# Moving three load buffers by 64 bytes: where an SBUF tile begins, and what the DMA engines make of it

## The chip, the cores and the metric

The kernel runs on one core of one Trainium2 chip. The metric is the device time in microseconds (us), the median of several runs of one program. Every run reported here is with a granted clock of 1.0.

## The reference

```python
def reference(x, axis):                 # x: 32 x 2048 x 2048 float32, about a tenth of it NaN; axis = -1
    return np.nanmax(x, axis=axis).astype(np.float32)
```

That is 65,536 rows of 2,048 floats: 537 MB are read, 0.26 MB are written, and the arithmetic is one pass.

## The kernel before

SBUF, the memory on the chip that the engines work in, has 128 *partitions* here. Data comes in by *tiles* of up to 28 x 512 floats per partition (57,344 bytes), into three load buffers in turn. Per piece of a tile, ACT (ScalarE) turns the upper half of every float into a 16-bit key in which NaN falls below everything, POOL (GpSimd; in some pieces ACT) writes the key back in its old form, and DVE (VectorE) takes the row maxima. The loads and stores are issued from SP (SyncE) and carried out by 16 DMA engines. All of it is hand-ordered with semaphores.

```python
    top = sing.tile([P, 1], f32, name="top")      # a bias for ACT
    warm = sing.tile([P, 1], f32, name="warm")    # loads ACT's table early: 1.28 us, done by 2.2; data from 5.8
    xts = [sing.tile([P, WIDE * D], i32, name=f"xt{i}") for i in range(BUFS)]      # 3 x 57,344 bytes
    kts = [sing.tile([P, KEYS], u16, name=f"kt{i}") for i in range(NKEYS)]         # 3 x 12,288 bytes
    accs = sing.tile([P, sum(rows)], f32, name="acc")
    # [cut]
                for c in loads:                   # one load for most tiles, several near the end
                    c *= Q
                    e = order.add("sp", nc.sync,
                        lambda: nc.sync.dma_start(
                            out=xt[:, at : at + c], in_=xg[:, base + at : base + at + c]),
                        before + lanes[turn], lane=f"load{turn}", step=16)
    # [cut: per piece ACT (Prelu) -> kt, POOL or ACT -> xt, DVE reduce -> acc]
                free[(number - 1) % BUFS] = after[-1:]    # the buffer is free after the last reduction
```

The built program lays the tiles one behind the other in each partition: four constants from byte 16,384 on, `top` at 16,512, `warm` at 16,544, and the first load buffer at 16,576, 64 x 256 + 192. The traces hold no addresses; these are those in the programs as built.

Of the kernel before, what the change touches and what calls it, by code (L numbers as in the profile page):

```python
# [49 lines left out]

KEYS = 3 * D
NKEYS = 3

LANES = 14

# [68 lines left out]
def kernel(  # L124
# [16 lines left out]
    P = nc.NUM_PARTITIONS  # L141
    f32, i32 = mybir.dt.float32, mybir.dt.int32
# [14 lines left out]
    sing = ctx.enter_context(tc.tile_pool(name="sing", bufs=1))  # L157
    flag = ctx.enter_context(
        tc.tile_pool(name="flag", bufs=1, space=bass.MemoryType.PSUM)
    )  # L160
    top = sing.tile([P, 1], f32, name="top")
    warm = sing.tile([P, 1], f32, name="warm")
    xts = [sing.tile([P, WIDE * D], i32, name=f"xt{i}") for i in range(BUFS)]
    kts = [sing.tile([P, KEYS], u16, name=f"kt{i}") for i in range(NKEYS)]
    accs = sing.tile([P, sum(rows)], f32, name="acc")
    nones = flag.tile([P, sum(rows)], i32, name="none")

    with tc.tile_critical():  # L168
# [16 lines left out]
        free = [[] for _ in range(BUFS)]  # L185
        kfree = [[] for _ in range(NKEYS)]
        key = 0
# [8 lines left out]
        for gi, (s, g) in enumerate(zip(rows, GROUPS)):  # L196
# [6 lines left out]
            for loads, pieces, reds in g:  # L203
# [26 lines left out]
                for c in pieces:  # L230
# [4 lines left out]
                    if used + c > KEYS:  # L235
                        key = (key + 1) % NKEYS
                        used = 0
                        kold, kfree[key] = kfree[key], []
                        if at + c == sum(loads) * Q:

                            kold = kold + kfree[(key + 1) % NKEYS]
                    kp = kts[key][:, used : used + c]
# [129 lines left out]
```

## Time and profile before

| what | value | how to read it |
|---|---|---|
| time | 1257.32 us (1257.19 to 1257.34, 4 runs) | these runs lie within 0.15 us; in later rounds one kernel's runs lie up to 1.0 us apart |
| DMA queue's transfer time | 99.3% of the 1255.5 us span | nearly without a pause |
| POOL, DVE, ACT busy | 93%, 89%, 79% | all below the DMA |
| full loads | 60, one every 16.940 us | the beat of the kernel up to about 1024 us |
| packets of 57,344 bytes | 7,680, median 2119 ns, mean 2120.7 ns | one DMA engine writing one partition's part of a full load |

Spacings and packet times here and below are worked out from the trace's record of every DMA packet (start, duration, size). A *packet* in that record is one descriptor: 109 loads x 128 partitions over 16 engines make 872 data packets per engine. The spacing is taken between the first packets of successive full loads.

### The profile page before, as it was taken

The numbers are of one execution on the slowest core, as the hardware profiler recorded it, in microseconds if no ns is written. First come the engines' busy times: TensorE is split into PE (matmuls) and PEld (weight loads), VectorE is DVE, ScalarE is ACT, GpSimd is POOL, SyncE is SP. The second block draws the span as 40 slices with busy tenths as digits, with TensorE's granted clock in tenths as the row PEclk, the third lists the DMA queues.
The fourth block names the chain that finished last, engine by engine and source line by source line (L and its number), as shares of the span: only waits on it lengthen the run. The fifth ranks groups of instructions, "written<-read, shape, count | busy, mean of one in ns | idle before, by whom it ended". The sixth has DMA issues, their size and how long they took to land.

```text
span 1255.5 us, 882 instructions
## 1 busy us (share of the span) xinstructions
DVE 1111.2 (89%) x180; ACT 987.6 (79%) x273; POOL 1168.4 (93%) x237
## 2 busy tenths in 40 slices
DVE  0888989888889988898988888898888899999999
ACT  3777887778787877788777877887777778889998
POOL 2999989998999899998999899989999999999997
DMA  9999999999999999999999999999999999999997
GB/s 413 438 435 413 438 438 438 437 431 418 438 438 435 435 417 438 438 435 437 435 418 438 438 433 438 420 433 438 435 437 437 417 436 426 438 428 428 426 421 281
DMA packets 16711, 537.20 MB, mean 428 GB/s; under 512 B 2752, under 2 KB 2752, under 8 KB 4160
## 3 DMA queue, kind: packets, MB, share of 16 engines
q1 hardware_dynamic: 16704, 537.14, 99.3%
q14 instruction: 7, 0.06, 0.0%
HBM read 536.87 MB, written 0.26 MB: 428 GB/s over the span
## 4 chain that ended last, share of the span: by engine, by line
DMA 42%; DVE 27%; POOL 18%; ACT 11%; SPq 1%; issue 1%; ACTq 0%
DMA xt<-in_x_dram 42%; DVE acc L180 27%; POOL xt L176 18%; ACT kt L172 10%; ACT xt L172 1%; SPq L214 1%; DVE xt L180 0%; DVE none L180 0%; SPq L367 0%; ACTq L111 0%; SPq L168 0%
## 5 line engine op out<-in xcount | busy, mean ns | idle before, releaser
L176 POOL TENSOR_SCALAR xt<-kt 128x4608 int16<-128x4608 uint16 (+10 forms) x233 | 1168.2, 5014 | 80.8 <-ACT kt L172 66.1
L180 DVE TENSOR_REDUCE acc<-xt 128x3 f32<-128x6144 f32 (+4 forms) x172 | 1108.0, 6492 | 140.4 <-POOL xt L176 130.4
L172 ACT ACTIVATE kt<-xt,top 128x3584 uint16<-128x3584 int16 (+8 forms) x252 | 937.0, 3756 | 260.6 <-DMA xt<-in_x_dram 238.8
L172 ACT ACTIVATE xt<-kt 128x3584 int16<-128x3584 uint16 (+5 forms) x19 | 51.3, 2701 | 0.6
L172 ACT ACT_TABLE_LOAD x1 | 1.3, 1283 | 0.9 <-SPq L168 0.9
L180 DVE TENSOR_REDUCE xt<-xt 128x1 f32<-128x1024 f32 x1 | 1.2, 1208 | 0.0
L180 DVE TENSOR_SCALAR none<-acc 128x428 int32<-128x428 f32 (+2 forms) x3 | 1.0, 339 | 0.1
L180 DVE TENSOR_TENSOR acc<-acc,none 128x428 int32<-128x428 int32 (+2 forms) x3 | 1.0, 332 | 0.1
L182 DVE MEMSET top<- 128x1 f32 x1 | 0.1, 59 | 1.0 <-SPq L168 1.0
L353 POOL MEMSET const-float32-0.0<- 128x1 f32 x1 | 0.1, 99 | 0.2 <-issue 0.2
L172 ACT ACTIVATE warm<-top 128x1 f32<-128x1 f32 x1 | 0.2, 202 | 0.0
L353 POOL MEMSET const-bfloat16-1.0<- 128x1 bf16 x1 | 0.1, 103 | 0.0
L353 POOL MEMSET const-uint8-127<- 128x1 uint8 x1 | 0.1, 103 | 0.0
L353 POOL MEMSET const-float32-1.0<- 128x1 f32 x1 | 0.1, 99 | 0.0
## 6 DMA issues: line engine op xcount, KB each, us to landing
xt<-in_x_dram SPq DMA_DIRECT2D x60, 7168.0 KB, 22.6
xt<-in_x_dram SPq DMA_DIRECT2D x3, 3840.0 KB, 15.1
xt<-in_x_dram SPq DMA_DIRECT2D x3, 3328.0 KB, 22.5
xt<-in_x_dram SPq DMA_DIRECT2D x8, 1024.0 KB, 27.3
xt<-in_x_dram SPq DMA_DIRECT2D x2, 4096.0 KB, 22.2
xt<-in_x_dram SPq DMA_DIRECT2D x2, 3584.0 KB, 20.3
xt<-in_x_dram SPq DMA_DIRECT2D x2, 3072.0 KB, 21.0
xt<-in_x_dram SPq DMA_DIRECT2D x3, 2048.0 KB, 31.1
```

What stands on the lines that cost most here:

```text
L172: return order.add("act", nc.scalar, lambda: nc.scalar.activation(**kw), deps)
L176: "pool", nc.gpsimd, lambda: nc.gpsimd.tensor_scalar(**kw), deps
L180: return order.add("dve", nc.vector, lambda: do(**kw), deps)
L182: e_top = order.add("dve", nc.vector, lambda: nc.vector.memset(top, EDGE), [])
L214: lambda: nc.sync.dma_start(out=xt[:, at : at + c], in_=xg[:, base + at : base + at + c]),
L353: nc = _bacc.Bacc("TRN2", target_bir_lowering=False, num_devices=1)
```

## The change

The two one-float tiles become one tile of 128 bytes, so that the three load buffers and all behind them begin on a multiple of 256 bytes. Nothing else changes.

```diff
+LEAD = 128
+
...
-    top = sing.tile([P, 1], f32, name="top")
-    warm = sing.tile([P, 1], f32, name="warm")
+
+    scalars = sing.tile([P, LEAD // 4], f32, name="scalars")
+    top, warm = scalars[:, 0:1], scalars[:, 1:2]
     xts = [sing.tile([P, WIDE * D], i32, name=f"xt{i}") for i in range(BUFS)]
```

## The prediction

> **What bounds the kernel now.** I read the page first (busy table, slices, DMA queue), then the groups by form, the chain of waits, the waits of the issuing queue, and a table of windows. The page says that three engines and the DMA are all nearly full:
>
> ```profile
> DVE 1111.2 (89%) x180; ACT 987.6 (79%) x273; POOL 1168.4 (93%) x237
> ...
> DMA  9999999999999999999999999999999999999997
> ...
> q1 hardware_dynamic: 16704, 537.14, 99.3%
> ...
> HBM read 536.87 MB, written 0.26 MB: 428 GB/s over the span
> ```
>
> The reader is to see that no compute engine reaches the share of the DMA queue: 99.3% of 1255.5 us is 1246.7 us of transfer time per DMA engine. It is a stream that hardly ever stops. The waits confirm it. Compute waits for data, and the queue waits for free buffers but early enough:
>
> ```profile
> ACT kt L172 <- DMA xt<-in_x_dram: 238.8, 66, 14.9
> DVE acc L180 <- POOL xt L176: 130.4, 57, 23.1
> POOL xt L176 <- ACT kt L172: 66.1, 72, 15.7
> ...
> SPq L214 <- DVE acc L180: 1156.9, 71, 37.9
> ```
>
> (engine and line, whom it waited for, us in total, times, longest). The issuing queue's 1156.9 us look alarming but cost nothing: a full load takes 22.6 us from issue to landing, yet loads land 16.94 us apart, so each is issued about 5.7 us before the previous one has landed, and the DMA engines go from one load straight to the next. In the steady part the timeline repeats the same pattern every 16.94 us:
>
> ```profile
> 595.56 15.15 DVE L180 TENSOR_REDUCE acc<-xt 128x4 f32<-128x8192 f32 x2 [1.79 <-POOL xt L176]
> 599.49 7.31 ACT L172 ACTIVATE kt<-xt,top 128x3584 uint16<-128x3584 int16 x2 [3.94 <-DMA xt<-in_x_dram]
> ...
> 612.50 15.15 DVE L180 TENSOR_REDUCE acc<-xt 128x4 f32<-128x8192 f32 x2 [1.80 <-POOL xt L176]
> 616.44 7.31 ACT L172 ACTIVATE kt<-xt,top 128x3584 uint16<-128x3584 int16 x2 [3.94 <-DMA xt<-in_x_dram]
> 619.81 16.77 POOL L176 TENSOR_SCALAR xt<-kt 128x3584 int16<-128x3584 uint16 x3 [0.19 <-ACT kt L172]
> ```
>
> Per tile ACT is idle 3.94 us waiting for the transfer, DVE 1.8 us, POOL 0.17 to 0.19 us. The transfer sets the pace, with POOL close behind: 16.77 us of a 16.94 us period. In one tile of eight ACT takes the 3584-element piece back from POOL (4.20 us), so POOL averages 16.77 - 4.20/8 = 16.24 us per tile. That is the real reserve, 4%.
>
> The end is different. The windows (us, then busy DVE, ACT, POOL, clock, DMA share, GB/s) show:
>
> ```profile
> 629.46:1003.00 373.54, 333.63 (x45) 288.03 (x68) 356.77 (x65) 1.00 1.00 434
> 1003.00:1130.00 127.00, 122.66 (x23) 106.01 (x29) 122.90 (x22) 1.00 1.00 428
> 1130.00:1180.00 50.00, 49.94 (x12) 49.22 (x19) 47.63 (x13) 1.00 1.00 428
> 1180.00:1230.00 50.00, 49.84 (x19) 47.01 (x27) 47.15 (x21) 1.00 1.01 422
> 1245.00:1248.00 3.00, 3.00 (x3) 3.00 (x4) 2.82 (x3) 1.00 0.27 63
> ```
>
> Until about 1130 us the DMA alone is full. From there to the end of the loads (about 1246 us) DVE is as full as the DMA (49.94 of 50). A faster transfer before 1130 us pulls this last part forward whole. A faster transfer after it mostly meets a busy DVE.
>
> [...] its packet records have a median of 312 ns for 8,192 bytes and 2119 ns for 57,344, so (2119 - 312) / (57,344 - 8,192) = 0.03676 ns per byte, 27.2 GB/s for one of 16 engines. [...] 15.15 to 15.16 us for each pair of DVE reductions through hundreds of microseconds of full transfer. I take from it that moving buffers should not change the engines' instructions.
>
> **The change part by part.** *Removed:* two tiles of one float each, which take 32 bytes apiece. With the four 32-byte constants ahead of them the first load buffer starts at byte 16,576 of a partition, 192 past a multiple of 256 (64 x 256 = 16,384). A load buffer is 57,344 = 224 x 256 bytes and a key buffer 12,288 = 48 x 256, so all of them share this phase. *Added:* one tile of 128 bytes that holds both floats: the first buffer moves up 64 bytes to 16,640 = 65 x 256, and everything behind with it. *Unchanged:* the number, form and order of instructions, the semaphores, the loads. The memset and the one-element activation at the start still act on one float. No instruction gets more elements, so compute cost is 0 us by count.
>
> What can move is one thing, the time of a load's descriptors. There are 109 loads of 128 partitions, thus 872 data descriptors per DMA engine, 480 of them of 57,344 bytes (60 full loads x 8).
>
> Size of what can be won: the first packets of successive full loads are 16.940 us apart (median from the packet records). Eight descriptors of 57,344 bytes at 27.2 GB/s are 16.866 us. The remainder is 0.074 us per load. [...]
>
> [...]
>
> The descriptors that count are those before 1130 us: the 60 full loads and about nine tiles of smaller ones, 69 x 8 = 552 (more where a tile is split, which I neglect). [...] After 1130 us I count at most another 0.5 us, because DVE is full there. The first load's arrival and the last reductions and stores keep their length.
>
> [...] I predict 1.0 us, **1256.3 us**.
>
> **The rivals.**
> *A: exactly nothing (1257.2 us).* [...]
> *B: [...] (1253 to 1254 us).* [...] Against: the first full loads, with the same placement, are spaced 16.914 us, 0.026 us closer than later ones, [...] unless the two act together. If they do act together (an ill-placed write that suffers only under load), the change could give it all.
> *C: POOL becomes the bound.* A period below about 16.8 us would meet POOL in seven of eight tiles. But the floor of the transfer alone is 16.866 us, so this cannot happen while POOL's instructions keep their length.
> *D: compute changes speed because its operands move too.* Read and written addresses of ACT, POOL and DVE all shift by 64 bytes. If POOL lost over 4% it would take the bound and time would rise by more than 1%; if it gained, nothing would be seen before 1130 us, and a little after. Nothing in the profile speaks for it: before and after the move, addresses are multiples of 64.
> *E: a larger gain than B*[...]. Against: 537.14 MB at 435.2 GB/s are 1234.2 us, and 1246.7 us of transfer time leave only 12.5 us even if every overhead vanished, 1.0% of the time. A gain over 2% from the transfer is out of reach.
>
> **Range and chances.** The three runs before lie within 0.15 us, so noise is small, and a run on another occasion may add some tenths. The upper end is rival A plus 0.5 us: 1257.8. The lower end is rival B with some of the tail's half microsecond: 1253.8. Faster by over 2% would need 25 us, twice what rival E leaves: 0.01. Slower by over 2% needs D at its worst: 0.01. Within 2%: 0.98.
>
> **What would show it right or wrong.** Right: full loads spaced slightly under 16.940 us and never under 16.866; the median of the 57,344-byte packets down from 2119 ns by 1 to 5 ns; the slope between packet sizes still 0.0368 ns per byte; POOL 3584, 4608 and 6144 pieces at 4200, 5341 and 7042 ns as before; DMA share still 99%. [...] the cap is wrong if the spacing goes under 16.866 us. The whole prediction is wrong if a compute group changes its mean by over 1%, or if the gap between transfers grows because buffers come free later.

The sum weighted three cases, one of them no gain at all with a weight of 0.4, the other two with 0.3 each; it came to about 1.1 us, taken down to 1.0. Of those two cases rival B is the larger. Two figures are estimates from the packet times: 16.866 us is eight packets of 57,344 bytes at the slope of 0.03676 ns per byte between the 312 and the 2119 ns, and 435.2 GB/s is 16 times the 27.2 of that slope.

## The result and the profile after

The changed kernel takes 1254.41 us (1254.32 to 1254.53, 4 runs) against 1257.32: **2.9 us less**, ratio 0.9977 (95% interval 0.996 to 0.9994). Ratios are the mean time of one kernel's fast runs over that of the other's in the same rounds, so not quite the ratio of the medians quoted. By the 2% verdict it is "same", but no run of one kernel comes near any run of the other.

Busy times, DMA slices and queue from the page of the kernel after:

```profile
DVE 1110.9 (89%) x180; ACT 987.4 (79%) x273; POOL 1168.2 (93%) x237
...
DMA  9999999999999999999999999999999999999996
...
q1 hardware_dynamic: 16704, 537.14, 99.3%
...
HBM read 536.87 MB, written 0.26 MB: 429 GB/s over the span
```

The engines' busy times are the same within 0.3 us. The queue's share is the same 99.3%, but of a span of 1252.5 us instead of 1255.5: the transfers take less time. The waits after (engine and line, whom it waited for, us in total, times, longest) say where the time came from:

```profile
ACT kt L175 <- DMA xt<-in_x_dram: 233.7, 61, 14.9
DVE acc L183 <- POOL xt L179: 128.1, 56, 23.0
POOL xt L179 <- ACT kt L175: 58.6, 40, 15.7
```

ACT waits 5.1 us less for data, and POOL 7.5 us less for ACT. A stretch of the steady part in the timeline after (start, us, engine and instruction, the idle time before it) shows it in one tile:

```profile
594.39 15.15 DVE L183 TENSOR_REDUCE acc<-xt 128x4 f32<-128x8192 f32 x2 [1.73 <-POOL xt L179]
598.30 7.31 ACT L175 ACTIVATE kt<-xt,scalars 128x3584 uint16<-128x3584 int16 x2 [3.92 <-DMA xt<-in_x_dram]
601.66 26.54 POOL L179 TENSOR_SCALAR xt<-kt 128x3584 int16<-128x3584 uint16 x5 [0.17 <-ACT kt L175]
...
615.20 7.31 ACT L175 ACTIVATE kt<-xt,scalars 128x3584 uint16<-128x3584 int16 x2 [3.89 <-DMA xt<-in_x_dram]
```

DVE and ACT instructions keep their 15.15 and 7.31 us; only the idle time before them shrinks by a few hundredths per tile (ACT's 3.94 to 3.89 or 3.92, DVE's 1.79 and 1.80 to 1.73 and 1.78). Tiles start 615.20 - 598.30 = 16.90 us apart. The same windows as before (us, then busy DVE, ACT, POOL, clock, DMA share, GB/s):

```profile
1130.00:1180.00 50.00, 50.00 (x12) 48.50 (x20) 47.48 (x14) 1.00 1.00 430
1180.00:1230.00 50.00, 49.93 (x20) 48.53 (x29) 47.72 (x21) 1.00 1.01 428
...
1245.00:1248.00 3.00, 2.97 (x3) 0.77 (x1) 0.63 (x1) 1.00 0.01 3
```

The loads are over before 1245 us, and DVE is busy for 50.00 and 49.93 of 50 us. The chain of work that ended last says the same for the stretch from 1130 us to the end. Before:

```profile
by line: DMA xt<-in_x_dram 49.3%; ACT kt L172 17.9%; DVE acc L180 16.2%; SPq L214 5.2%; POOL xt L176 3.5%; ACT xt L172 2.9%; issue 1.7%; DVE xt L180 0.9%; DVE none L180 0.1%; ACTq L111 0.0%
```

and after:

```profile
by line: DVE acc L183 94.1%; issue 4.4%; DVE xt L183 1.0%; DVE none L183 0.4%
```

After the change the end hangs on DVE alone.

From the packet records of both:

| | before | after |
|---|---|---|
| packets of 57,344 bytes: mean, median, share at exactly 2116 ns | 2120.7, 2119 ns, 12% | 2116.3, 2116 ns, 98% |
| packets of 8,192 bytes, median | 312 ns | 309 ns |
| excess of before, by packet size: 4,096 / 10,240 / 30,720 / 57,344 bytes | 3.7 / 3.9 / 3.8 / 4.4 ns | |
| spacing of full loads, median | 16.940 us | 16.909 us |

Two things are to be seen. The excess hardly grows with the size of the packet from 4,096 bytes on (3.6 to 5.2 ns over all these sizes), so it is not paid by the byte or by each 256 bytes. And after the change nearly every full packet has one and the same duration, while before nine in ten are scattered from 2116 to 2126 ns.

How the gain builds up, in landing times of loads counted from the landing of the first one:

| load landed | before, us | after, us | ahead, us |
|---|---|---|---|
| 5th | 67.77 | 67.66 | 0.11 |
| 21st | 339.51 | 338.51 | 1.00 |
| 41st | 678.46 | 677.11 | 1.36 |
| 61st (last full load) | 1017.90 | 1015.50 | 2.40 |
| 74th | 1127.93 | 1124.99 | 2.94 |
| 109th (last) | 1241.10 | 1237.11 | 3.98 |

The loads finish 4.0 us earlier and the kernel 2.9 us earlier. The other 1.1 us is swallowed at the end, where DVE is full. (The spacing is that of the first packet of each load, thus of the engine that is furthest ahead; a load has 16 landings in the trace, and its time here is the last of them. The 16 lie 0.41, 1.06, 1.17 and 1.77 us apart for the 5th, 21st, 41st and 61st load before, and 0.31, 0.57, 0.98 and 1.19 us after. That is why the lead grows unevenly, and by more than 0.031 us per load.)

### The profile page after: what moved, and what is told of

It reads as the page before. It is cut to its first block, busy times and chain, and to the rows that moved or that the text cites. A ratio compares the mean times of both kernels' runs of the same rounds, so it can differ in the third digit from the quotient of the medians.

```text
span 1252.5 us, 882 instructions
## 1 busy us (share of the span) xinstructions
DVE 1110.9 (89%) x180; ACT 987.4 (79%) x273; POOL 1168.2 (93%) x237
## 3 DMA queue, kind: packets, MB, share of 16 engines
q1 hardware_dynamic: 16704, 537.14, 99.3%
## 4 chain that ended last, share of the span: by engine, by line
DMA 36%; DVE 32%; POOL 21%; ACT 10%; issue 1%; SPq 0%
DMA xt<-in_x_dram 36%; DVE acc L183 32%; POOL xt L179 21%; ACT kt L175 9%; ACT xt L175 1%; DVE xt L183 0%; DVE none L183 0%; SPq L217 0%; SPq L370 0%; SPq L171 0%
## 5 line engine op out<-in xcount | busy, mean ns | idle before, releaser
L175 ACT ACTIVATE kt<-xt,scalars 128x3584 uint16<-128x3584 int16 (+8 forms) x252 | 936.8, 3755 | 256.8 <-DMA xt<-in_x_dram 233.7
```

The costliest lines, as they stand in the source:

```text
L175: return order.add("act", nc.scalar, lambda: nc.scalar.activation(**kw), deps)
```

## The experiments

The theory (**1**): the DMA engines pay for writes whose start in SBUF is off a multiple of 256. Its rivals: the joined tile did it (**2**); the key buffers and results had to move, so it is compute (**3**); the loss arises only where compute and DMA use the memory at once (**4**); it is a mismatch of source and destination (**5**). Within theory 1 the *size* is open: a price that grows with the distance from the multiple, one price wherever the start is, or something else. Twelve kernels ran, each in 5 rounds with runs of the kernel before on the same chip (bare_on has 4 timed runs).

### Where the start lies: past192, past64, past128, mult512

Edit: only the size of the shared tile, to 64, 192, 256 and 384 bytes.

```diff
-LEAD = 128
+LEAD = 64     # past192; 192: past64; 256: past128; 384: mult512
```

> The kernel after with its shared tile cut from 128 to 64 bytes, so that everything behind it begins 192 bytes past a multiple of 256, as in the kernel before. Theory 1 (the start of the load buffers costs the DMA engines time) and its rival 'compute operands moved' both expect the time of before, 1257.3 us, spacing of full loads 16.94 us. The rival 'the joined tile of two floats did it' expects 1254.4 us.

> Shared tile of 192 bytes: all begins 64 bytes past a multiple of 256. Theory 1 [...] expects a third of the loss, about 1255.4 us. [...] If only the 128-byte boundary counts: also 1257.3 us.

> Shared tile of 256 bytes: all begins 128 bytes past a multiple of 256. [...] 'Only multiples of 128 count': 1254.4 us.

> Shared tile of 384 bytes: load buffers begin at a multiple of 512 (the kernel after: at an odd multiple of 256; each of its buffers is 224 x 256 long, so all three are alike). Theory 1 with 256 as the unit: 1254.4 us, 57,344-byte packets at 2116 ns. If 512 is the unit: faster by up to 1 us.

(A price in proportion to the distance would give a third of the loss at 64, 1255.4 us, and two thirds at 128, 1256.3 us; one price wherever the start is, 1257.3 us in both.)

| start modulo 256 | time, us | ratio to before (95%) | 57,344-byte packets, mean ns | spacing, us |
|---|---|---|---|---|
| kernel before: 192 | 1257.14 | 1 | 2120.7 | 16.940 |
| past192: 192 | 1257.12 | 1.0 (0.9988 to 1.0013) | 2120.7 | 16.940 |
| past64: 64 | 1257.10 | 1.0 (0.9987 to 1.0012) | 2120.7 | 16.942 |
| past128: 128 | 1257.08 | 1.0 (0.9986 to 1.0013) | 2120.5 | 16.940 |
| mult512: 0 | 1254.34 | 0.9978 (0.9966 to 0.9991) | 2116.3 | 16.909 |

The time of the kernel before and the packets of the first row are from its own runs here and its trace above. past192 has the changed code at the old place and the old time: rival 2 falls. 64, 128 and 192 cost the same, so the loss does not follow the distance from the multiple. A multiple of 512 brings nothing over an odd multiple of 256: of the starts tried, 256 is the unit. Every load is a multiple of 2,048 bytes long, so the end of each write moves with its start; the runs do not part the two.

### Which tiles: loads_on_keys_off, keys_on_loads_off

```diff
+    sing.tile([P, 48], f32, name="pad")       # loads_on_keys_off (LEAD 128): keys and results 192 past
+    sing.tile([P, 16], f32, name="pad")       # keys_on_loads_off (LEAD 64): keys and results at a multiple
     kts = [sing.tile([P, KEYS], u16, name=f"kt{i}") for i in range(NKEYS)]
```

> Load buffers at a multiple of 256 as in the kernel after, but a pad of 192 bytes puts the key buffers and the results 192 past one, as in before. Theory 1 (only the DMA's writes matter): 1254.4 us. Rival 'key buffers and results matter': nearer to 1257.3 us.

> The opposite: load buffers 192 past a multiple of 256, key buffers and results on one. Theory 1: 1257.3 us, full loads 16.94 us apart. Rival: nearer to 1254.4 us.

With only the load buffers on multiples of 256: 1254.33 us, ratio 0.9977 (0.9964 to 0.9991). With only the keys and results on them: 1257.13 us, ratio 1.0 (0.9987 to 1.0012). The whole effect goes with the load buffers; where keys and results begin is worth nothing that these runs can show. (The profiled run of the first of the two was 1255.25 us: 64 packets over 2.2 us where the kernel after has 5, most of them around the sixth to tenth full load. Its spacing is 16.909 us from there on.)

### Without any compute: bare_on, bare_off

All activations, POOL instructions and reductions are cut. A load waits for the load three before it in the same buffer, and the stores write zeros. Their outputs are wrong, which doesn't matter for the times. `bare_off` has LEAD 64, thus 192 past.

```diff
-                [cut: the pieces, from "clean = []" to the last "after.append(e)"]
-                free[(number - 1) % BUFS] = after[-1:]
+                after = [e for _, _, e in landed]
+                free[(number - 1) % BUFS] = after
```

> The loads alone, at multiples of 256, each waiting only for the load three before it in the same buffer; no activations, no POOL, no reductions, and a memset and the stores as result (wrong on purpose). Theory 1 without any part of compute: full loads 16.90 to 16.91 us apart and packets of 2116 ns, about 1243 us.

> The loads alone with the buffers 192 past a multiple of 256 (wrong on purpose). If the loss lies in the DMA engines themselves: packets spread over 2116 to 2126 ns and about 4 us longer than the loads alone at multiples of 256. If it arises only where compute uses the same memory: the same time as those, packets at 2116 ns.

1247.25 us on multiples, 1251.06 us off them: **3.8 us apart**. The page of bare_on:

```profile
span 1245.4 us, 183 instructions
...
q1 hardware_dynamic: 16704, 537.14, 99.8%
```

and that of bare_off:

```profile
span 1249.3 us, 183 instructions
...
q1 hardware_dynamic: 16704, 537.14, 99.8%
```

The queue's share is 99.8% in both, so the longer span is longer transfers, with no engine at work beside them. Packets have means of 2116.2 and 2120.4 ns, spacings of 16.909 and 16.940 us: the figures of the full kernels. Rival 4 falls: the loss needs no compute. The 3.8 us agree with 872 packets x 4.2 ns = 3.7 us and with the 4.0 us by which the last load of the changed kernel lands earlier. My 1243 us for bare_on was a lapse: it is the transfer time of one engine alone, without start, last landing and stores.

### Source or destination: bare_src_off, bare_both_off

```diff
+                    sh = 48 if c == 28 * Q and base + at + c < s * D else 0     # 48 floats = 192 bytes
-                            in_=xg[:, base + at : base + at + c]
+                            in_=xg[:, base + at + sh : base + at + sh + c]
```

56 of the 60 full loads are shifted; the others would read past their partition's part of the input. A price for such reads: a time above the 1247.25 us of the loads alone would have spoken for one.

> The loads alone, buffers at multiples of 256, but nearly all full loads read from 192 bytes further on in the source (wrong on purpose). [...] If only writes pay: 1247.25 us.

> The loads alone with buffers 192 past a multiple of 256 and full loads read from 192 bytes further on (wrong on purpose), so that source and destination are alike within 256 bytes. If the loss is a mismatch between the two: near 1248 us (only the smaller loads, still unequal, lose). If it is the start of the write as such: 1251 us, or more if the read pays too.

With the source alone shifted: 1247.53 us, packets at a median of 2116 and a mean of 2116.1 ns, spacing 16.909 us. With both shifted: 1251.27 us, mean 2120.5 ns, spacing 16.940 us. Shifting the source does nothing to the packets in either case (0.3 and 0.2 us in the time, within the spread of those runs). The loss is no mismatch (rival 5 falls). It goes with the place of the write.

### How the loss is dealt out: one_off, past16

Each load buffer gets 256 spare bytes and begins at a chosen byte of them: (0, 192, 0) in one_off, (16, 16, 16) in past16.

```diff
-    xts = [sing.tile([P, WIDE * D], i32, name=f"xt{i}") for i in range(BUFS)]
+    wide = [sing.tile([P, WIDE * D + 64], i32, name=f"xt{i}") for i in range(BUFS)]
+    xts = [t[:, o : o + WIDE * D] for t, o in zip(wide, (0, 48, 0))]     # past16: (4, 4, 4)
```

> Only the second of the three load buffers is moved, to 192 past a multiple of 256 (through 256 spare bytes in each buffer); the other two stay on multiples. If each ill-placed descriptor pays for itself: a third of the loss, about 1255.3 us, packets into the second buffer 2116 to 2126 ns and the others at 2116 ns. If an ill-placed load also disturbs the next ones: more than half of the loss, slow packets in all three buffers.

> All three load buffers begin 16 bytes past a multiple of 256[...]. If any start off a multiple of 256 costs one and the same: 1257.1 us. [...]

(The other expectation: a time over the kernel before by 1 us or by far more.)

**one_off met neither expectation.** It takes 1254.62 us against 1257.24 for the kernel before (ratio 0.9979, 0.9966 to 0.9993), 2.6 us less where the change itself gives 2.9 and mult512 2.8. One ill-placed buffer of three costs some 0.2 to 0.3 us, a tenth of the loss and not a third, and even that is hardly clear of the noise. Its full packets: 98% at 2116 ns in all three buffers, the ill-placed one included; spacing 16.909 us. So an ill-placed write has no fixed price of its own. The loss comes when ill-placed loads follow one another.

The starts of the traces fit that. Spacings of the first full loads in bare_off, in us:

```
16.909 16.910 16.912 16.922 16.946 16.938 16.940 16.940 16.949 16.945
```

The first three are as short as with a good placement. From the fifth to the eighth on the spacing stays near 16.94, and does so in every kernel with all buffers 64, 128 or 192 past. The packets show the step more sharply: in each of these kernels the first four full loads have a median of 2116 ns, and from the fifth on 2119 to 2121 ns. (With the small first load, which is ill-placed too, five loads are free of the loss.)

The end of one_off shows the same. Its last tile comes in eleven loads, all into the ill-placed buffer. Mean packets of these loads, in ns:

| load of the last tile | 1st | 2nd | 3rd | 4th | 5th | 6th | 7th | 8th | 9th | 10th | 11th |
|---|---|---|---|---|---|---|---|---|---|---|---|
| bytes per packet | 6,144 | 10,240 | 8,192 | 2,048 | 6,144 | 6,144 | 6,144 | 4,096 | 4,096 | 2,048 | 2,048 |
| kernel after | 234.0 | 385.0 | 309.0 | 84.0 | 234.0 | 234.0 | 234.0 | 159.0 | 159.0 | 84.0 | 84.0 |
| one_off | 234.0 | 385.0 | 309.0 | 84.0 | 235.5 | 238.1 | 237.8 | 162.3 | 163.1 | 86.1 | 87.3 |
| kernel before | 237.0 | 389.1 | 313.8 | 84.8 | 240.3 | 238.2 | 237.8 | 162.3 | 163.0 | 86.1 | 87.1 |

Four ill-placed loads in a row cost nothing, the fifth a part, and from the sixth on packets are as slow as in the kernel before. An earlier tile of four loads into that buffer also costs nothing. So what counts seems to be the number of ill-placed loads in a row, some four or five, whether they bring 57,344 bytes per partition or 2,048 to 10,240. Why it takes so many, and how few well-placed loads in between keep the loss away, no run tells. Runs with two of three buffers off, or with fewer packets at a time, would be next.

**past16** takes 1258.87 us, ratio 1.0013 (1.0001 to 1.0026), 1.6 us more than the kernel before. Packets have a mean of 2122.7 ns, 2.0 ns over those of the kernel before and 6.4 over those of the kernel after, and 872 x 2.0 ns = 1.7 us. A start 16 bytes past a multiple costs a little more than the others tried, and not by the byte: the mean is 2.1 ns over the kernel before at 6,144 and at 10,240 bytes, and 2.0 at 57,344. Here only the first two full loads have a median of 2116 ns. The engines do not mind: from its page,

```profile
span 1256.9 us, 882 instructions
...
DVE 1111.3 (88%) x180; ACT 987.9 (79%) x273; POOL 1167.9 (93%) x237
```

busy times are those of the kernel before within 0.5 us.

No run beats the kernel after clearly; mult512 and loads_on_keys_off equal it.

## Why the prediction was right or wrong

**The bound** held: a change that touches only the transfers moved the time, and bare_on and bare_off show the transfers' 1247 and 1251 us as the floor under 1254 and 1257.

**The cost per byte** did not move: it is (2116 - 309) / 49,152 = 0.03676 ns after the change, as before, and the excess is flat over packet sizes. That only a cost per descriptor could be won back was the assumption, not shown beforehand.

**"Compute cost is 0 us by count"** held: busy times within 0.3 us, the POOL pieces of 3584, 4608 and 6144 elements at 4200, 5341 and 7039 ns. Rivals C and D of the prediction did not occur.

**The cap** held. The spacing fell to 16.909 us, not under 16.866 (an estimate from the slope), which gives back 0.031 us of the remainder of 0.074 us, 3.9 ns per descriptor; the mean packet fell by 4.4 ns.

**The term that was mis-sized** is the placement's share of that remainder: the weighting came to about 1 us, and the measured gain is 2.9, the size of the largest case, which I gave 0.3. The equal size is in part luck: that case took 552 descriptors at a price that no trace showed, while 74 x 8 = 592 had run when the lead reached 2.9 us, and full packets lost 4.4 ns. Two steps led there. First, the price per packet in the middle case was too small, and only assumed: the packets lost 4.4 ns. A price that grows with the distance from the multiple was no better: 64, 128 and 192 cost the same. Second, I read the shorter spacing of the first loads (16.914 us, 0.026 us or 3.3 ns per packet less) as a sign of something else than the placement, "unless the two act together". The exception was the truth. The first loads with a bad placement are fast because too few ill-placed ones have gone before, as the first loads of every such trace and the last ones of one_off suggest, and with a good placement the later ones are as fast (16.909).

**The end** was right in kind: the loads gained 2.9 us by the 74th, which is also the gain of the whole, and the further 1.0 us that they gained until the last one brought nothing. I had allowed it up to half a microsecond.

One reading in the prediction holds only in part: POOL's 16.24 us per tile, a reserve of 4%, is that of the first 48 full loads. In the last 12, ACT takes no piece back, and POOL has 16.77 us of each period; it still did not become the bound.

## What to carry to other kernels

Where a kernel is bound by its loads, try load buffers that begin on multiples of 256 bytes (and are multiples of 256 long, so that all share the start): here it cost 64 bytes and brought 2.9 us of 1257, a quarter of a per cent but clear of the noise. Look at the scatter of equal packets in the trace: here 98% had one duration with the good placement and 12% with the bad. Look at packets by load, not only at their mean: that the loss starts with the fifth load tells more than its size. And the last part of this kernel, where DVE was full as well, gained nothing from the faster stream.
